# Other places for a decoder step's index-stage buffers, banks and weight halves, and its last normalization on VectorE

## The chip, the cores and the metric

The kernel runs on one core of a Trainium2 chip. Its engines are TensorE (PE, matmuls and transposes into the eight banks of PSUM), VectorE (DVE), ScalarE (ACT, activations by loadable function tables), GpSimd (POOL) and SyncE (SP), which here only issues transfers. Each engine works through its own instruction queue in order; semaphores order the engines against each other. The metric is the time of one execution on the device in microseconds (us).

## What is computed

The reference is one layer of a hybrid decoder for a prompt of 1024 tokens and for 8 sequences with 4 new tokens each and 8192 cached keys. One normalized input is projected by one wide matrix into two branches:

```python
h = rmsnorm(x, g_pre); z = h @ w_in       # qa ka va | qi ki wi | ga | qb kb vb gb
# A: sparse attention
score = sum_h wi[h] * relu(qi[h] @ ki.T / 8)          # 8 index heads, causal
idx = top_k(score, 256)                               # keys kept per query
oa = softmax(qa @ ka[idx].T / 8 + bias) @ va[idx]     # 8 heads, 2 key/value heads
# B: retention, 8 heads, chunks of 128
ob = causal_decay(rope(qb) @ rope(kb).T / 8) @ vb + carried_state
y = concat(silu(ga) * oa, silu(gb) * head_norm(ob)) @ w_out
x = x + rmsnorm(y, g_post)
x = x + (p @ w_ple_up) * sigmoid(x @ w_ple_gate)
```

`head_norm` subtracts each head's mean and multiplies by the reciprocal root of its variance. Outputs are the new `x` for prompt and samples, the new keys, values and index keys, and the final retention states. All is float32; a projection is made of three matmuls on operands split into a high part and a rest (`hi`, `lo`).

## The kernel before

**How orders come about.** The program is traced line by line in one function. A planner then writes each engine's order from estimated costs: at each point an engine takes the first traced instruction that it estimates to be ready, wherever it stands in the program, and buffers and semaphores are assigned along with it. `tc.issue_after(ins)` keeps what its block traces on the engine of `ins` behind `ins` in that queue. Transfers are issued on SP's queue in its order, indirect ones (gathers) on POOL's. A tile of a pool has a `tag` and a number `bufs` of buffers; a new tile of a tag waits until the oldest of its buffers is no longer read.

**Stages.** The span begins with norms and index projections, then index scores of the prompt. From about 155 to 292 us runs the *index stage*, the loop over 8 sequences `b` and 2 halves `a`. It loads a slab of cached index keys (`key_pages`, `kx`, an indirect transfer on POOL, two buffers), transposes it on DVE (L913), multiplies it by the sequence's index queries into a pair of banks (`pox`, L920), takes the relu on ACT (`rl`, L925), and one iteration later sums the heads (`head_sum`: `py`, L881 and L884, copied by ACT into `ys` at L886). In between it steps the prompt's bisection for the top 256 (`bp`: counts on DVE, L740, and on ACT, `js`, L738), and steps `units()`: projection units, each three matmuls times eight input blocks for one group of tokens, in the order queries (`qa0`, `qa1`), keys and values (`kava`), gates (`ga0`, `ga1`), three groups for each of two column halves.

PSUM has, in this phase, two pairs (tag `S`), two banks of tag `b` and two of tag `t`. Projections (`pb`) and head sums (`py`) take `b`; small transposes (`kvt`) and flags take `t`.

A key or value unit copies its projection from the bank into one half of the tile `kvs` (`use_kv`, L466, one buffer) and appends its second part to the list `turn`. The next unit first runs that part (`turn_kv`): transposes of the copy on TensorE (`kvt`, L475), a copy into the other half of `kvs` (L477) and the stores of it (L479, L498). A gate unit applies Silu on ACT (`sga`, L503) and stores the result.

Weights come by `load_w`: two raw halves of four blocks (`wraw`, two buffers), each converted by one cast on ACT (`whi`, L202) and four subtractions on POOL (`wlo`, L203). `lazy=True` returns the conversion as a generator to be stepped later; without it, it is traced at once. `ga0` and `ga1` are traced at once, as units reach them.

**Retention** follows (292 to about 560 us), four head pairs `hp`, with the samples' search for their top 256 beside it. The fourth pair's outputs and gates are stored raw (`yr_d`), with each head's mean and variance kept in `lmv`.

**Attention** of the prompt (about 561 to 735 us) loops over 8 query blocks `qb` and 2 key/value heads `kv`: score matmuls (`sa`, L1835 and L1836), bias, mask and least value on DVE (L1841, `latest[0]`), exponential on ACT (L1845), transposes (`ptp`), copies (`pT`), products with the values (`ob`). Beside it run the samples' attention (`sa` generator: gathers on POOL) and the last pair's normalization, the generator `ln = last_norm()`. It is stepped once ahead of the loop, once in each of the first two blocks, and then three times per `qb` and `kv` from `qb` 2 on. `last_roots` adds the epsilons, takes a root on ACT (L1247) and, a step later, its reciprocal with one Newton round on DVE. Then for each of 9 token blocks: load into `dn` (one buffer, L1791), two steps on normalize on DVE (L1797), multiply by the gate on POOL (L1799), store (L1800).

```python
        for t in range(9):
            a = at.tile([128, 2, 128], F32, tag="dn", bufs=1, name="dn")
            nc.sync.dma_start(a[:n], yr_d[:n, t])
            ...
            nc.gpsimd.tensor_tensor(a[:n, 0, :], a[:n, 0, :], a[:n, 1, :], op=ALU.mult)
            nc.sync.dma_start(yb_d[:n, t, 3, :], a[:n, 0, :])
```

At `qb` 3 the post-norm gains are loaded for the merge (`gpost`, L1814, 512 KB). The **merge** ends the program: output projection (`po`), second norm, gate and embedding.

Of the kernel before, what the change touches and what calls it, by code (L numbers as in the profile page):

```python
# [11 lines left out]
F32 = mybir.dt.float32  # L12
F32R = mybir.dt.float32r
BF16 = mybir.dt.bfloat16
I32 = mybir.dt.int32
# [8 lines left out]
NS = 32  # L24
# [109 lines left out]
def tile_step(ctx: ExitStack, tc: tile.TileContext, I, O):  # L134
# [25 lines left out]
    def bank(name, tag="b"):  # L160
        if tag in kept.get("tags", ()):
            return kept["pool"].tile([128, 512], F32, tag="s", bufs=1, name=name)
        of = psum["apart" if tag == psum["tag"] else "pool"]
        return of.tile([128, 512], F32, tag=tag, bufs=psum["bufs"][tag], name=name)
# [6 lines left out]
    def C(name, rows=128):  # L171
        o, w = _CW[name]
        return cst[:rows, o:o + w]
# [48 lines left out]
    def wcols(*cols):  # L222
        return [(w_in[:, c:c + n], n) for c, n in cols]
# [210 lines left out]
    def key_pages(i):  # L434

        b, a = i // 2, i % 2
        kx = slab("kx").bitcast(F32).rearrange("p a b -> p (a b)")
        paged[0] = nc.gpsimd.indirect_dma_start(
            out=kx[:, :2048], out_offset=None, in_=pages,
            in_offset=bass.IndirectOffsetOnAxis(ap=kidx[:, a * 8 + b:a * 8 + b + 1], axis=0)).ins  # L440
        return kx
# [20 lines left out]

    def use_kv(g, pt, outs, outp, new, then=lambda tk: None):

        st = sx.tile([128, 2, 416], F32, tag="kvs", bufs=1, name="kvs")
        nc.scalar.copy(st[:, 0, :GRP[g][1]], pt[:, :GRP[g][1]])  # L466
        turn.append(lambda: then(turn_kv(g, st, outs, outp, new)))

    def turn_kv(g, st, outs, outp, new):

        t0, n = GRP[g]
        tp = bank("kvt", "t")
        for i in range(0, n, 128):
            rows = min(128, n - i)
            nc.tensor.transpose(tp[:rows, i:i + 128], st[:, 0, i:i + rows], ident)  # L475
        nb = NP[g]
        nc.scalar.copy(st[:, 1, :nb], tp[:, :nb])  # L477
        tk = st[:, 1, :nb].rearrange("p (b c) -> p b c", c=128)
        nc.sync.dma_start(outp[0, 0, t0:t0 + nb].rearrange("(b p) n d -> p b (n d)", p=128), tk)  # L479
        if g == SG:  # L480
            nc.vector.tensor_copy(new, tp[:NS, 384:512])
            nc.sync.dma_start(outs.rearrange("o b t n d -> (o b t) (n d)"), new)
        return tk
# [15 lines left out]

    def use_ga(j, g, pt):  # L500
        t0, n = GRP[g]
        sg = qsp.tile([128, 2, 416], F32, tag="qst", bufs=2, name="sga")
        nc.scalar.activation(sg[:, 0, :n], pt[:, :n], AF.Silu)  # L503
        nc.sync.dma_start(ga_d[:, j, t0:t0 + n], sg[:, 0, :n])

    def units():

        def triple(w, c0, use):
            for g in range(3):
                while turn:  # L510
                    turn.pop(0)()
                proj_b(w, c0, 128, use, (g,))
                yield

        w.extend([load_w("qa0", wcols((QA, 256))), load_w("qa1", wcols((QA + 256, 256)))])
        loads = [("kava", KA), ("ga0", GA), ("ga1", GA + 256), None]
        for i in range(5):
            for a in range(2):
                use = ((lambda g, pt: use_qa(2 * i + a, g, pt)) if i < 2 else
                       (use_ka, use_va)[a] if i == 2 else  # L520
                       (lambda g, pt: use_ga(2 * i - 6 + a, g, pt)))
                yield from triple(w[i], a * 128, use)
            if i < 3:
                w.append(load_w(loads[i][0], wcols((loads[i][1], 256)), late=0 if i else 3))

    w = []
    unit_gen = units()
    tick = [0.0]

# [322 lines left out]

    sp_one = cp.tile([128, 1], F32, name="sp_one")
    nc.gpsimd.memset(sp_one, 1.0)
    bp = bisect_prompt()

    def step(gen, n=1):
# [7 lines left out]
    for up in range(2):  # L865
        nc.vector.tensor_tensor(wst[:, up], wcol[:, :, None].to_broadcast([128, 8, 32]),
                                C(f"wsel{up}")[:, None, :].to_broadcast([128, 8, 32]), op=ALU.mult)
    pn = bank("pn", "t")
    for h in range(8):
        nc.tensor.matmul(pn[:NS, h * 32:h * 32 + 32], qsn[:, h, :], kis, start=True, stop=True)  # L870
# [5 lines left out]
    nc.vector.tensor_tensor(newsc, newsc, C("nfill", 32), op=ALU.add)  # L876
    pend = []
    def head_sum(b, rls):
        py = bank("py")

        last_ = nc.tensor.matmul(py[96:128, :], wst[:, 1, b, :], rls[3], start=True, stop=True)  # L881
        with tc.issue_after(last_.ins):
            for i in range(3):
                nc.tensor.matmul(py[32 * i:32 * i + 32, :], wst[:, i % 2, b, :], rls[i], start=True, stop=True)  # L884
        ys = sx.tile([128, 512], F32, tag="ys", bufs=2, name="ys")
        nc.scalar.copy(ys, py)  # L886
        nc.sync.dma_start(xt_d[b], ys)
        pend.append(lambda: by_key(b, ys))
# [17 lines left out]
    for b in range(8):  # L906
        rls = []
        for a in range(2):
            kx = key_pages(2 * b + a) if b else kxs[a]
            po = pair("pox")  # L910
            kT = (kx[:, 2048:], kx[:, :1024])
            for up in range(2):
                nc.vector.transpose(kT[up], kx[:, up * 1024:up * 1024 + 1024])  # L913
            head = None
            for up in (1, 0):
                for u2 in range(2):
                    for r in range(2):
                        o, rr = 32 * (2 * (r ^ up) + u2), slice(r * 64, r * 64 + 64)
                        with (tc.issue_after(head) if head else ExitStack()):
                            mm = nc.tensor.matmul(po[o:o + 32, up * 512:up * 512 + 512], qbd[rr, b, :],  # L920
                                                  kT[up][rr, u2 * 512:u2 * 512 + 512], start=True, stop=True,
                                                  tile_position=(64 * r, o))
                        head = head or mm.ins
            rl = sx.tile([128, 1024], F32, tag="rl", bufs=3, name="rl")
            nc.scalar.activation(rl, po, AF.Relu)  # L925
            rls += [rl[:, :512], rl[:, 512:]]
            later()
            tickb[0] += 1.25
            while tickb[0] >= 1:
                tickb[0] -= 1  # L930
                step(bp)
            with tc.issue_after(scored[1]):
                unit((2, 2.5, 2, 2)[2 * b + a] if b < 2 else 12.5 / 12)
        pend.append(lambda b=b, rls=rls: head_sum(b, rls))
# [305 lines left out]

    def last_roots():

        v = wif[:, 54:72]
        z = at.tile([128, 18], F32, name="lz")
        nc.vector.tensor_tensor(v.rearrange("p (t h) -> p t h", h=2),
                                lmv[:, :, 1].rearrange("p (t h) -> p t h", h=2), epsn[:, :, 6:8], op=ALU.add)
        nc.scalar.activation(lrs, v, AF.Sqrt)  # L1247
        yield
        with tc.issue_after(latest[0]):
            nc.vector.reciprocal(lrs, lrs)  # L1250
            nc.vector.tensor_tensor(z, lrs, lrs, op=ALU.mult)
            nc.vector.tensor_tensor(z, z, v, op=ALU.mult)
            nc.vector.tensor_scalar(z, z, -0.5, 1.5, op0=ALU.mult, op1=ALU.add)
            nc.vector.tensor_tensor(lrs, lrs, z, op=ALU.mult)

    smask = C("smask", 32)
    bmask = C("bmask")
# [526 lines left out]

    def last_norm():

        yield from last_roots()
        for t in range(9):
            n = 128 if t < 8 else NS
            a = at.tile([128, 2, 128], F32, tag="dn", bufs=1, name="dn")  # L1790
            nc.sync.dma_start(a[:n], yr_d[:n, t])  # L1791
            yield
            yield
            with tc.issue_after(latest[0]):
                for j in range(2):
                    i, js = 2 * t + j, slice(j * 64, j * 64 + 64)
                    nc.vector.tensor_scalar(a[:n, 0, js], a[:n, 0, js], lmv[:n, i, 0:1], lrs[:n, i:i + 1],  # L1797
                                            op0=ALU.subtract, op1=ALU.mult)
            nc.gpsimd.tensor_tensor(a[:n, 0, :], a[:n, 0, :], a[:n, 1, :], op=ALU.mult)  # L1799
            nc.sync.dma_start(yb_d[:n, t, 3, :], a[:n, 0, :])  # L1800
            yield

    latest = [None]
    ln = last_norm()
    caus = C("caus")
    next(ln)

    for qb in range(8):
        qas = qnext
        if qb < 7:  # L1810
            qnext = load_q(qb + 1)
            if qb == 3:
                with tc.issue_after(last_q[0]):
                    nc.sync.dma_start(gpost, I["g_post"].to_broadcast([128, D]))  # L1814
        n = (qb + 1) * 128
# [4 lines left out]
        for kv in range(2):  # L1820
# [26 lines left out]
                more(0.4 + n / 1200)  # L1847
            if qb > 1:
                step(ln)
            elif qb == kv:  # L1850
                next(ln)
            ob = bank("ob", "o")
            for kb in range(qb + 1):
                if kb == 1 and qb > 1:
# [247 lines left out]
```

## Time and profile before

| | |
|---|---|
| median of 3 runs | 974.04 us (972.46 to 976.85) |
| profiled execution | 971.68 us, span 969.9 us |
| mean granted TensorE clock | 0.984 |
| busy: PE, PEld, DVE, ACT, POOL | 95%, 81%, 66%, 47%, 33% |
| moved by DMA | 104.40 MB, 108 GB/s mean |

The span is what the trace covers, from the first to the last instruction; the profiled execution's own time is a little longer. PEld is the loading of stationary operands, which overlaps the matmuls. The granted clock is the share of full speed at which TensorE ran. A row of waits has the engine and line that waited, the one that released it, microseconds in total, times, and the longest. A row of a timeline has start, duration, engine, line, operation, output and inputs, and in brackets the idle time of the engine just ahead and what ended it.

### The profile page before, as it was taken

Reading aid. Unit: us, or ns where it says so; the run is one execution under the profiler, and the core shown is the slowest. Engines: PE = TensorE matmul, PEld = TensorE weight load, DVE = VectorE, ACT = ScalarE, POOL = GpSimd, SP = SyncE. Lnnn points to the kernel's source line nnn. Section 1 sums busy time; section 2 is a strip of 40 time slices with the busy share of each in tenths; the row PEclk is TensorE's granted clock in tenths of the full one; section 3 lists DMA queues with packets and bytes.
Section 4 is the critical chain, followed back from the end, with each engine's and each line's share of the span. In section 5 each row is a group of like instructions: output and inputs, shape, how many; then the busy total and the mean of one; then the engine's idle time right before and its main releaser. Section 6 shows DMA issues by size and latency. Waiting matters only on the chain.

```text
span 969.9 us, 19199 instructions
## 1 busy us (share of the span) xinstructions
PE 917.9 (95%) x7108; PEld 786.8 (81%) x7108; DVE 639.4 (66%) x1898; ACT 458.5 (47%) x1022; POOL 318.8 (33%) x442
## 2 busy tenths in 40 slices
PE   3999999888999999999999988999999999999998
PEld 2988788656779988899889965666668999999998
DVE  6837867878835669978888387877754234943332
ACT  5635654666323886425334284556555334422210
POOL 4205112312415414515344076545204422033300
PEclk8999999988999999999999999999999999999999
DMA  8413224676545110332145445433113222612211
GB/s 261 132 66 83 92 77 153 226 231 197 205 145 124 45 45 24 81 84 63 45 129 164 115 122 167 136 101 103 38 35 87 88 68 77 191 49 94 89 35 39
DMA packets 102129, 104.40 MB, mean 108 GB/s; under 512 B 22002, under 2 KB 92210, under 8 KB 99602
## 3 DMA queue, kind: packets, MB, share of 16 engines
q1 hardware_dynamic: 96274, 76.94, 26.8%
q0 software_dynamic: 5760, 26.22, 8.6%
q8 instruction: 56, 0.92, 0.4%
q14 instruction: 39, 0.32, 0.1%
HBM read 80.38 MB, written 22.76 MB: 106 GB/s over the span
## 4 chain that ended last, share of the span: by engine, by line
PE 54%; DVE 6%; issue 5%; DMA 3%; ACT 2%; POOL 1%; SPq 0%; DVEq 0%; ACTq 0%; POOLq 0%
PE pg L298 3%; PE pg L300 3%; PE pg L299 3%; PE ob L1866 3%; PE ptp L1858 3%; PE po L298 3%; PE po L300 3%; PE po L299 3%; PE pvg L299 2%; PE pvg L298 2%; PE pvg L300 2%; PE sa L1835 2%; PE pqk L298 2%; PE pqk L299 2%; PE pqk L300 2%
## 5 line engine op out<-in xcount | busy, mean ns | idle before, releaser
L1317 POOL DMA_INDIRECT kvs<-in_cache_kv,idx x64 | 67.5, 1054 | 81.8 <-PE pkg L1534 18.5
L298 PE MATMUL pvg<-whi_vgb,xh 128*128 128x256 f32 x256 | 75.2, 294 | 0.5 <-DVE rp L1153 0.5
L299 PE MATMUL pvg<-wlo_vgb,xh 128*128 128x256 f32 x256 | 73.5, 287 | 0.8 <-POOL wlo_vgb L203 0.8
L299 PE MATMUL pqk<-wlo_qkb,xh 128*128 128x256 f32 x256 | 73.9, 289 | 0.0
L298 PE MATMUL pqk<-whi_qkb,xh 128*128 128x256 f32 x256 | 73.8, 288 | 0.1
L300 PE MATMUL pvg<-whi_vgb,xl 128*128 128x256 f32 x256 | 73.7, 288 | 0.0
L300 PE MATMUL po<-whi_o,yTl 128*128 128x256 f32 x256 | 73.1, 285 | 0.4 <-POOL yTl L1914 0.4
L298 PE MATMUL po<-whi_o,yTh 128*128 128x256 f32 x256 | 73.2, 286 | 0.0
L299 PE MATMUL po<-wlo_o,yTh 128*128 128x256 f32 x256 | 72.9, 285 | 0.0
L298 PE MATMUL pg<-whi_g,yTh 128*128 128x256 f32 x256 | 72.8, 285 | 0.0
L300 PE MATMUL pqk<-whi_qkb,xl 128*128 128x256 f32 x256 | 72.8, 284 | 0.0
L300 PE MATMUL pg<-whi_g,yTl 128*128 128x256 f32 x256 | 72.4, 283 | 0.0
L299 PE MATMUL pg<-wlo_g,yTh 128*128 128x256 f32 x256 | 72.3, 283 | 0.0
L1845 ACT ACTIVATE L<-L,mn 128x128 f32<-128x128 f32 (+7 forms) x64 | 49.6, 776 | 22.5 <-DVE mn L1841 22.5
L2057 DVE TENSOR_TENSOR sgm<-pu,sgm 128x256 f32<-128x256 f32 x32 | 13.6, 424 | 64.4 <-PE pu L300 61.1
L203 POOL TENSOR_TENSOR wlo_g<-wraw_g,whi_g 128x256 fp32r<-128x256 f32 x32 | 27.2, 882 | 87.1 <-ACT whi_g L202 87.0
L1858 PEld LDWEIGHTS ptp<-cst,L 128*128 128x128 f32 x288 | 31.6, 142 | 23.8 <-issue 19.4
L298 PEld LDWEIGHTS po<-whi_o,yTh 128*128 128x128 f32 x256 | 49.1, 192 | 2.0 <-issue 1.6
L298 PEld LDWEIGHTS pvg<-whi_vgb,xh 128*128 128x128 f32 x256 | 48.4, 189 | 2.6 <-PE pvg L307 0.8
L298 PEld LDWEIGHTS pg<-whi_g,yTh 128*128 128x128 f32 x256 | 48.8, 191 | 1.6 <-issue 1.2
L569 DVE SCALAR_TENSOR_TENSOR score<-r,wi,score 128x384 f32<-128x384 f32 (+5 forms) x42 | 41.3, 984 | 13.1 <-ACT r L568 10.8
L300 PEld LDWEIGHTS po<-whi_o,yTl 128*128 128x128 f32 x256 | 49.1, 192 | 0.6 <-POOL yTl L1914 0.6
(536 smaller groups left out, 3058.7 us busy)
## 6 DMA issues: line engine op xcount, KB each, us to landing
wraw_qkb<-in_w_in SPq DMA_DIRECT2D x16, 256.0 KB
wraw_vgb<-in_w_in SPq DMA_DIRECT2D x16, 256.0 KB
qas<-qas_d SPq DMA_DIRECT2D x8, 512.0 KB
wraw_o<-in_w_out SPq DMA_DIRECT2D x8, 512.0 KB
xr<-in_x_prompt SPq DMA_DIRECT2D x8, 512.0 KB
wraw_g<-in_w_ple_gate SPq DMA_DIRECT2D x8, 512.0 KB
out_y_prompt<-sgm SPq DMA_DIRECT2D x32, 128.0 KB
qas_d<-qst SPq DMA_DIRECT2D x8, 384.0 KB
```

Of the source, the lines that this page charges most:

```text
L203: nc.gpsimd.tensor_tensor(lo[:, k, :n], raw, hi[:, k, :n].bitcast(F32), op=ALU.subtract)
L298: nc.tensor.matmul(pt[:, :n], ah, hi[:, k, :n], start=(k == 0), stop=False)
L299: nc.tensor.matmul(pt[:, :n], ah, lo[:, k, :n], start=False, stop=False)
L300: nc.tensor.matmul(pt[:, :n], al, hi[:, k, :n], start=False, stop=(k == kc - 1))
L569: nc.vector.scalar_tensor_tensor(sc, r[:, :n], wi[:, qb, h:h + 1], sc if h else place[:, :n], op0=ALU.mult, op1=ALU.add)
L1317: return nc.gpsimd.indirect_dma_start(out=dst, out_offset=None, in_=kvflat, in_offset=bass.IndirectOffsetOnAxis(ap=idx, axis=0))
L1835: nc.tensor.matmul(s[:, :wc], qas[:, h, :], kah[kv][:, c:c + wc], start=True, stop=False)
L1845: behind[0] = nc.scalar.activation(L[:, :n], L[:, :n], AF.Exp, bias=least, scale=-1.0, accum_out=sm[:, i4:i4 + 1])
L1858: nc.tensor.transpose(tp[:, i4 * 128:i4 * 128 + 128], P[i4][:, kb * 128:kb * 128 + 128], ident)
L1866: nc.tensor.matmul(ob[64 * o:64 * o + 64, :256], vtok[:, kb, kv * 64:kv * 64 + 64], pT[:, o * 256:o * 256 + 256], start=(kb == 0), stop=(k ...
L2057: nc.vector.tensor_tensor(sg[:rows], usrc, sg[:rows], op=ALU.mult)
```

## The change

It has four parts.

- Keys and values: `kvs` is split into `kva` (two buffers) and `kvb` (one); the list `turn` holds a count, so that the transposes are traced two units after the copy instead of one. `sga` loses an unused half.
- Gate weights: `ga0` and `ga1` are loaded lazily; at each slab of the index stage, two blocks of each unfinished conversion are traced behind the slab's issue, and what is left is traced ahead of the first gate unit.
- `py` takes a `t` bank. A Silu of one column is traced ahead of the index loop.
- Last pair: `last_roots` takes the reciprocal root on DVE, from a shifted bit pattern and three Newton rounds, a step each. `last_norm` alternates between `dn` and the constant table `slots` (which nothing reads any more by then) and loads a block ahead. The gate product runs on DVE, and the store is traced a step later. The generator is first stepped at `qb` 2. `gpost` is loaded at `qb` 5.

```diff
     def use_kv(g, pt, outs, outp, new, then=lambda tk: None):
-        st = sx.tile([128, 2, 416], F32, tag="kvs", bufs=1, name="kvs")
-        nc.scalar.copy(st[:, 0, :GRP[g][1]], pt[:, :GRP[g][1]])
-        turn.append(lambda: then(turn_kv(g, st, outs, outp, new)))
+        st = sx.tile([128, 416], F32, tag="kva", bufs=2, name="kva")
+        nc.scalar.copy(st[:, :GRP[g][1]], pt[:, :GRP[g][1]])
+        turn.append([2, lambda: then(turn_kv(g, st, outs, outp, new))])
...
-        nc.scalar.copy(st[:, 1, :nb], tp[:, :nb])
+        kb = sx.tile([128, 384], F32, tag="kvb", bufs=1, name="kvb")
+        nc.scalar.copy(kb[:, :nb], tp[:, :nb])
...
             for g in range(3):
-                while turn:
-                    turn.pop(0)()
+                for t in turn:
+                    t[0] -= 1
+                while turn and not turn[0][0]:
+                    turn.pop(0)[1]()
...
         for i in range(5):
+            if i > 2:
+                for _ in w[i][3]:
+                    pass
...
-                w.append(load_w(loads[i][0], wcols((loads[i][1], 256)), late=0 if i else 3))
+                w.append(load_w(loads[i][0], wcols((loads[i][1], 256)), lazy=i > 0, late=0 if i else 3))
+                if i:
+                    halves.append(w[-1][3])
...
+    nc.scalar.activation(sp_two, sp_one, AF.Silu)
...
-        py = bank("py")
+        py = bank("py", "t")
...
             kx = key_pages(2 * b + a) if b else kxs[a]
+            with tc.issue_after(paged[0]):
+                for half in halves:
+                    step(half, 2)
...
     def last_roots():
-        nc.vector.tensor_tensor(v.rearrange("p (t h) -> p t h", h=2),
-                                lmv[:, :, 1].rearrange("p (t h) -> p t h", h=2), epsn[:, :, 6:8], op=ALU.add)
-        nc.scalar.activation(lrs, v, AF.Sqrt)
-        yield
         with tc.issue_after(latest[0]):
-            nc.vector.reciprocal(lrs, lrs)
-            nc.vector.tensor_tensor(z, lrs, lrs, op=ALU.mult)
-            nc.vector.tensor_tensor(z, z, v, op=ALU.mult)
-            nc.vector.tensor_scalar(z, z, -0.5, 1.5, op0=ALU.mult, op1=ALU.add)
-            nc.vector.tensor_tensor(lrs, lrs, z, op=ALU.mult)
+            V.tensor_tensor(v.rearrange("p (t h) -> p t h", h=2),
+                            lmv[:, :, 1].rearrange("p (t h) -> p t h", h=2), epsn[:, :, 6:8], op=ALU.add)
+        V.tensor_scalar(lrs.bitcast(I32), v.bitcast(I32), 1, None, op0=ALU.logical_shift_right)
+        V.tensor_scalar(lrs.bitcast(I32), lrs.bitcast(I32), -1.0, float(0x5F3759DF), op0=ALU.mult, op1=ALU.add)
+        for _ in range(3):
+            yield
+            with tc.issue_after(latest[0]):
+                V.scalar_tensor_tensor(z, lrs, -0.5, lrs, op0=ALU.mult, op1=ALU.mult)
+            V.tensor_tensor(z, z, v, op=ALU.mult)
+            V.scalar_tensor_tensor(lrs, z, 1.5, lrs, op0=ALU.add, op1=ALU.mult)
...
     def last_norm():
+        def load(t):
+            a = rows2[t % 2]
+            n = 128 if t < 8 else NS
+            nc.sync.dma_start(a[:n], yr_d[:n, t])
+            return a[:n]
+        rows2 = [at.tile([128, 2, 128], F32, tag="dn", bufs=1, name="dn"),
+                 C("slots").rearrange("p (a b) -> p a b", a=2)]
+        after = load(0)
         yield from last_roots()
         for t in range(9):
-            a = at.tile([128, 2, 128], F32, tag="dn", bufs=1, name="dn")
-            nc.sync.dma_start(a[:n], yr_d[:n, t])
-            yield
+            a, after = after, load(t + 1) if t < 8 else None
             yield
...
-            nc.gpsimd.tensor_tensor(a[:n, 0, :], a[:n, 0, :], a[:n, 1, :], op=ALU.mult)
-            nc.sync.dma_start(yb_d[:n, t, 3, :], a[:n, 0, :])
+            nc.vector.tensor_tensor(a[:, 0, :], a[:, 0, :], a[:, 1, :], op=ALU.mult)
+            yield
+            nc.sync.dma_start(yb_d[:n, t, 3, :], a[:, 0, :])
             yield
...
-    next(ln)
...
-            if qb == 3:
+            if qb == 5:
                 with tc.issue_after(last_q[0]):
                     nc.sync.dma_start(gpost, I["g_post"].to_broadcast([128, D]))
...
             if qb > 1:
                 step(ln)
-            elif qb == kv:
-                next(ln)
```

More of the change, by code (lines that the diff above doesn't have):

```diff
@@ L474, in turn_kv @@
             rows = min(128, n - i)
-            nc.tensor.transpose(tp[:rows, i:i + 128], st[:, 0, i:i + rows], ident)
+            nc.tensor.transpose(tp[:rows, i:i + 128], st[:, i:i + rows], ident)
         nb = NP[g]
-        nc.scalar.copy(st[:, 1, :nb], tp[:, :nb])
-        tk = st[:, 1, :nb].rearrange("p (b c) -> p b c", c=128)
+        kb = sx.tile([128, 384], F32, tag="kvb", bufs=1, name="kvb")
+        nc.scalar.copy(kb[:, :nb], tp[:, :nb])
+        tk = kb[:, :nb].rearrange("p (b c) -> p b c", c=128)
         nc.sync.dma_start(outp[0, 0, t0:t0 + nb].rearrange("(b p) n d -> p b (n d)", p=128), tk)
@@ L501, in use_ga @@
         t0, n = GRP[g]
-        sg = qsp.tile([128, 2, 416], F32, tag="qst", bufs=2, name="sga")
-        nc.scalar.activation(sg[:, 0, :n], pt[:, :n], AF.Silu)
-        nc.sync.dma_start(ga_d[:, j, t0:t0 + n], sg[:, 0, :n])
+        sg = qsp.tile([128, 416], F32, tag="qst", bufs=2, name="sga")
+        nc.scalar.activation(sg[:, :n], pt[:, :n], AF.Silu)
+        nc.sync.dma_start(ga_d[:, j, t0:t0 + n], sg[:, :n])
     def units():
@@ L523, in units @@
             if i < 3:
-                w.append(load_w(loads[i][0], wcols((loads[i][1], 256)), late=0 if i else 3))
-    w = []
+                w.append(load_w(loads[i][0], wcols((loads[i][1], 256)), lazy=i > 0, late=0 if i else 3))
+                if i:
+                    halves.append(w[-1][3])
+    w, halves = [], []
     unit_gen = units()
@@ L854, in tile_step @@
     nc.gpsimd.memset(sp_one, 1.0)
+    sp_two = cp.tile([128, 1], F32, name="sp_two")
     bp = bisect_prompt()
@@ L1241, in last_roots @@
     def last_roots():
-        v = wif[:, 54:72]
+        V, v = nc.vector, wif[:, 54:72]
         z = at.tile([128, 18], F32, name="lz")
-        nc.vector.tensor_tensor(v.rearrange("p (t h) -> p t h", h=2),
-                                lmv[:, :, 1].rearrange("p (t h) -> p t h", h=2), epsn[:, :, 6:8], op=ALU.add)
-        nc.scalar.activation(lrs, v, AF.Sqrt)
-        yield
         with tc.issue_after(latest[0]):
-            nc.vector.reciprocal(lrs, lrs)
-            nc.vector.tensor_tensor(z, lrs, lrs, op=ALU.mult)
-            nc.vector.tensor_tensor(z, z, v, op=ALU.mult)
-            nc.vector.tensor_scalar(z, z, -0.5, 1.5, op0=ALU.mult, op1=ALU.add)
-            nc.vector.tensor_tensor(lrs, lrs, z, op=ALU.mult)
+            V.tensor_tensor(v.rearrange("p (t h) -> p t h", h=2),
[8 more added lines that the diff above has]
+            V.scalar_tensor_tensor(lrs, z, 1.5, lrs, op0=ALU.add, op1=ALU.mult)
     smask = C("smask", 32)
@@ L1796, in last_norm @@
                     i, js = 2 * t + j, slice(j * 64, j * 64 + 64)
-                    nc.vector.tensor_scalar(a[:n, 0, js], a[:n, 0, js], lmv[:n, i, 0:1], lrs[:n, i:i + 1],
+                    nc.vector.tensor_scalar(a[:, 0, js], a[:, 0, js], lmv[:n, i, 0:1], lrs[:n, i:i + 1],
                                             op0=ALU.subtract, op1=ALU.mult)
-            nc.gpsimd.tensor_tensor(a[:n, 0, :], a[:n, 0, :], a[:n, 1, :], op=ALU.mult)
-            nc.sync.dma_start(yb_d[:n, t, 3, :], a[:n, 0, :])
+            nc.vector.tensor_tensor(a[:, 0, :], a[:, 0, :], a[:, 1, :], op=ALU.mult)
+            yield
+            nc.sync.dma_start(yb_d[:n, t, 3, :], a[:, 0, :])
             yield
```

## Prediction

> **What bounds the kernel now.** I read the page's first two parts, then the windows by stage, then the waits of the stages in which TensorE is not full, then the timelines of single stalls.
>
> ```profile
> span 969.9 us, 19199 instructions
> PE 917.9 (95%) x7108; PEld 786.8 (81%) x7108; DVE 639.4 (66%) x1898; ACT 458.5 (47%) x1022; POOL 318.8 (33%) x442
> ```
>
> TensorE is the bound over the whole span: 917.9 of 969.9 us. The change takes no matmul out, so it can only win TensorE's idle time, 52.0 us, or its lost clock. The windows by stage say where that lies (columns: length, then busy time of PE, PEld, DVE, ACT and POOL, granted clock, DMA share, GB/s).
>
> ```profile
> 164.00:246.00 82.00, 69.61 (x482) 52.28 (x483) 67.73 (x170) 49.55 (x85) 21.69 (x29) 0.92 0.67 218
> 292.00:560.00 268.00, 263.67 (x2258) 242.15 (x2259) 203.44 (x736) 129.60 (x334) 102.90 (x188) 1.00 0.32 83
> 564.00:580.00 16.00, 11.98 (x93) 9.09 (x93) 14.54 (x64) 13.87 (x43) 14.31 (x15) 1.00 0.44 122
> 580.00:600.00 20.00, 20.00 (x173) 13.20 (x171) 15.63 (x65) 11.22 (x33) 15.51 (x15) 1.00 0.57 170
> 608.00:672.00 64.00, 63.67 (x490) 42.79 (x485) 50.51 (x188) 40.07 (x84) 32.52 (x36) 1.00 0.40 114
> ```
>
> The first row is the index stage (key pages, query/key/gate projections, the prompt's bisection): 12.4 us idle, clock 0.92. The second, retention, loses 4.3. Attention begins near 561 and is loose in its first 16 us (4.0 idle, with ACT and DVE nearly full) and again just before 604. Both loose stages are what the diff touches. The waits of the first:
>
> ```profile
> PE kvt L475 <- ACT kvs L466: 3.7, 2, 2.4
> PE py L881 <- ACT sga L503: 3.5, 1, 3.5
> PE pox L920 <- DVE kx L913: 2.2, 1, 2.2
> PE pb L288 <- DVE qst L379: 2.0, 2, 1.3
> ACT kvs L466 <- DMA out_k_prompt<-kvs: 3.7, 2, 2.5
> POOL kx L438 <- PE pox L920: 28.8, 4, 10.1
> ```
>
> **The change part by part: index stage.** *Key/value transposes.* Today a projection group's copy into `kvs` waits for the former group's store out of the same tile (3.7 us on ACT), and the transposes one unit later wait for that copy: 3.7 us of TensorE in two waits. With two `kva` buffers, a separate `kvb`, and the transposes two units late, the copy has a whole unit more and no store in front of it. I take -3.7 (between -3.7 and 0). The wait for the store moves to the second copy (into the single `kvb`), behind which `rl`, `js` and `ys` queue on ACT; the next projection covers it as long as no second tenant of the banks comes within it.
>
> *Bank of the head sums.* `py` takes a `b` bank, which it shares with the projections, so it waits for the gate's activation. That one was late because ACT was held by a count that waited for DVE, and then loaded a table:
>
> ```profile
> 225.89 1.15 ACT L738 ACTIVATE js<-score,W 128x1024 bf16<-128x1024 f32 x1 [3.79 <-DVE W L771]
> 227.15 1.28 ACT L503 ACT_TABLE_LOAD   x1
> 228.44 0.49 ACT L503 ACTIVATE sga<-pb 128x384 f32<-128x384 f32 x1
> 228.00:232.00 4.00, 3.02 (x12) 1.34 (x13) 1.89 (x9) 3.96 (x8) 0.00 (x0) 0.53 0.94 300
> 232.00:236.00 4.00, 4.00 (x15) 3.85 (x15) 3.69 (x12) 3.10 (x6) 0.42 (x1) 0.61 0.95 304
> ```
>
> In a `t` bank `py` no longer waits for the gate: -3.5 (to 0). After that gap the clock falls to 0.53 and 0.61, which costs 0.47 x 3.02 + 0.39 x 4.00 = 3.0 us of matmul time; if the gap goes, so does this: -3.0 (to 0).
>
> *What is late next.* Saving 10.2 leaves 71.8 us of stage for 67.73 us of DVE work that doesn't shrink: 94% full, in order, with page transposes, bisection and PSUM splits behind each other. The waits on DVE (2.2 for pages, 2.0 for query splits) stay, and more will show. The amount is not in the trace; its ends are 0 and 10.2 (all given back). I take the middle, +5.1, since DVE is nearer to full than to its present 83%. Stage: -10.2 + 5.1 = -5.1.
>
> *Gate weights in halves.* The conversions move behind each page's issue on POOL, two at a time, instead of eight in a row:
>
> ```profile
> 178.24 5.57 POOL L203 TENSOR_TENSOR wlo_ga<-wraw_ga,whi_ga 128x256 fp32r<-128x256 f32 x8 [6.69 <-ACT whi_ga L202]
> L290 PE MATMUL pb<-xh,wlo_ga x96: 279/336/548, 220.4 to 289.8; 128*128 128x384 f32 x32, 128*128 128x416 f32 x32, 128*128 128x256 f32 x32
> ```
>
> They end at 183.8 and TensorE first reads them at 220.4: 36.6 us of cover. Page issues stop waiting up to 5.6 us behind them, which only matters where pages are late (in the +5.1). 0. The cost if the cover goes is the slower rival below.
>
> *The early Silu.* It is meant to load the table ahead of the gates. But an instruction whose operands are ready runs as soon as its engine is free, wherever it stands in the program: the memset of its source, from line 854, ran at 0.99 us.
>
> ```profile
> 0.99 0.10 POOL L854 MEMSET sp_one<- 128x1 f32 x1
> 5.85 0.20 ACT L270 ACTIVATE ry_x<-rv_x 128x1 f32<-128x1 f32 x1 [0.22 <-DVE rv_x L267]
> 6.87 0.16 DVE L275 TENSOR_TENSOR ry_x<-ry_x,rz_x 128x1 f32<-128x1 f32 x1
> 8.60 1.28 DVE L599 SCALAR_TENSOR_TENSOR x<-x,ry_x,mask 128x1024 f32<-128x1024 f32 x1 [1.32 <-DMA mask<-in_g_pre]
> ```
>
> I expect it near 2 us too: a load that the root at 5.85 undoes with a second one. That delays the root by 1.28, its chain ends at 7.03 + 1.28 = 8.31, and the scaling waits for `g_pre` until 8.60 anyway: 0 (at most 1.28). The load at 227 then stays, but TensorE no longer stands behind it through `py`: 0.
>
> **Attention.** *Loads a step ahead.* One `dn` buffer serves load, normalization, gate product and store in turn:
>
> ```profile
> 595.49 0.65 SPq L1814 DMA_DIRECT2D gpost<-in_g_post  x1
> 596.23 0.38 SPq L1791 DMA_DIRECT2D dn<-yr_d  x1
> 602.72 0.54 DVE L1797 TENSOR_SCALAR dn<-dn,wi 128x64 f32<-128x64 f32 x2 [6.00 <-DMA dn<-yr_d]
> 603.80 0.77 PE L1835 MATMUL sa<-kahi,qas 128*128 128x512 f32 x1 [3.60 <-DVE mn L1841]
> 604.00:608.00 4.00, 4.00 (x16) 2.14 (x17) 3.68 (x13) 2.56 (x8) 3.27 (x3) 0.61 0.32 90
> ```
>
> The load left behind the 512 KB of `gpost`, DVE stood 6.00 us at its head, the score banks were not drained, TensorE waited 3.60 and then ran at 0.61 (0.39 x 4.00 = 1.6). With two buffers each load has three steps of lead, and `gpost` goes two blocks later, where nothing needs it until the merge. -5.2, the surest term (at least -3.6).
>
> *SP's queue.* The stores now follow a step behind their product, so SP no longer stands at them:
>
> ```profile
> SPq L1800 <- POOL dn L1799: 40.0, 9, 13.3
> SPq L1791 <- DMA yb_d<-dn: 8.7, 6, 2.7
> ```
>
> Queries and gates queued behind those stores are loaded a block ahead; TensorE shows no wait on them: 0. Each load still waits for the store that empties its buffer, now a step old; 2.7 at most and hidden.
>
> *Roots.* Before, ACT switches tables twice for one root:
>
> ```profile
> 569.56 1.28 ACT L1247 ACT_TABLE_LOAD   x1
> 570.86 0.22 ACT L1247 ACTIVATE wi<-wi 128x18 f32<-128x18 f32 x1
> 571.57 1.28 ACT L1845 ACT_TABLE_LOAD   x1
> 571.60 0.65 PE L1534 MATMUL pkg<-cst,kvs 128*128 128x128 f32 x4 [0.55 <-ACT kgT L1535]
> 573.41 1.10 PE L1858 MATMUL ptp<-cst,L 128*128 128x128 f32 x3 [0.68 <-ACT L L1845]
> 576.50 0.66 PE L1534 MATMUL pkg<-cst,kvs 128*128 128x128 f32 x4 [0.61 <-ACT kgT L1535]
> ```
>
> 2 x 1.28 + 0.22 = 2.8 us leave ACT where it is nearly full; TensorE's waits for ACT there sum to 1.84. DVE is as full (14.54 of 16), so I take -1.0 (0 to -1.84). The Trainium skill, "ScalarE: Activation LUTs", section "What ACT_TABLE_LOAD costs", adds a drain of about 1.38 us to each load; by it 5.5 us would leave ACT, and the term would go to its end, -1.84. Here the root starts 0.02 us after its load ends, so the trace shows no drain.
>
> *DVE's new work.* Added: twelve small instructions for the roots (sum, shift, constant, three rounds of three) and nine gate products; removed: six small ones. Their prices:
>
> ```profile
> 572.80 0.17 DVE L1251 TENSOR_TENSOR lz<-wi 128x18 f32<-128x18 f32 x1
> 575.31 0.71 DVE L1252 TENSOR_TENSOR lz<-lz,wi 128x18 f32<-128x18 f32 x1
> L1797 DVE TENSOR_SCALAR dn<-dn,wi x18: 285/310/519, 587.1 to 670.4; 128x64 f32<-128x64 f32 x16, 32x64 f32<-32x64 f32 x2
> ```
>
> The two root rows are the same shape, 0.17 alone and 0.71 while POOL converts. Net 6 x (0.17 to 0.71) + 9 x (0.31 to 0.52) = 3.8 to 8.9 us, spread from about 580 to 700. DVE is free there for 4.4 us in 580 to 600 and 13.5 in 608 to 672. Mostly hidden; +1.0 (0 to +8.9). The Trainium skill, "SBUF — State Buffer", section on the shared port pair, says that DVE with two SBUF inputs and a GpSimd instruction that reads SBUF block each other in full; by it the price would be the 8.9 end wherever POOL computes. The 0.71 row agrees.
>
> **Sum.** -5.1 - 5.2 - 1.0 + 1.0 = -10.3 us. The profiled execution took 971.68 (span 969.9 and 1.78 around it): 961.4. It lies 2.4 below the median of the runs, 974.04; against the median that is 963.7, my forecast.
>
> **The rivals.** *The index stage gives all back.* If DVE paces that stage, PE's idle time only changes its names: attention's -5.2 alone, 968.8. For it: DVE at 67.73 of 82.00. Against: 14 us of it are free, and the two longest waits are on ACT.
>
> *The orders are dealt anew.* Each engine's order is a planner's, from estimated costs, so early edits reorder what follows. The 292 to 560 stage waits for only 4.3 us now; if it and the pages waited 7 us more, twice the longest stall of the index stage, little is left: 971.
>
> *Slower: the gate weights come late.* The last pair of each weight's conversions is now queued on POOL behind a page issue, which waits for its slab until TensorE has read an earlier page: up to 10.1 us. If TensorE gets to the gate projection first, it stands for that wait. Two weights: 20.2 - 10.3 = +9.9, so 984. It decides once the 36.6 us of cover are used up; two such issue waits in a row would take 20.2 of them.
>
> **How the numbers follow.** Forecast 963.7 with its own range 957 to 968.5: 0.50. More (nothing given back): 0.05. Attention alone, 968.8: 0.18, on the edge of what can be told from no change, 0.5% or 4.9 us (969.2): two thirds of it counts as faster. Dealt anew, 971: 0.14. Slower: 0.13. So faster 0.62 (a little under the sum, 0.67, since 968.8 is so near the edge), same 0.24, slower 0.14. The range 956 to 977: down to the stage without give-back (963.7 - 5.1 - 0.84 - 1 = 956.8), up past the two middle rivals; it leaves out the slower one and the extremes.
>
> **What would show it.** Right: no wait of `kvt` on ACT's copy, none of `py` on `sga`; the clock near 1.00 in 225 to 240; DVE above 90% in the index stage; no 6 us wait on `dn`; one table load (not three) between 563 and 575; the early Silu's table load near 2 us and a second root-table load near 6. Wrong: waits of `pb` on `wlo_ga`, of `kvt` or `py` on `ys` or `kvb` copies, longer waits on `kx`, or new idle time between 292 and 560.

## The result, and the profile after

The changed kernel takes 961.46 us (median of 6 runs, 959.65 to 963.53), the kernel before beside it 973.6 (6 runs, 971.54 to 976.85): ratio 0.9878, 95% interval 0.9851 to 0.9904, so 1.2% faster. The profiled execution took 961.63. Its page has the same 7108 matmuls and 5.6 us less TensorE time on them:

```profile
span 959.9 us, 19189 instructions
PE 912.3 (95%) x7108; PEld 781.4 (81%) x7108; DVE 642.1 (67%) x1913; ACT 457.6 (48%) x1022; POOL 308.5 (32%) x433
```

The window of the index stage that the prediction showed for before, and TensorE's waits between 157 and 292 us, in the changed kernel:

```profile
164.00:246.00 82.00, 76.95 (x563) 59.22 (x562) 73.04 (x174) 51.99 (x90) 23.98 (x32) 0.98 0.73 239
```
```profile
PE pox L933 <- issue: 3.5, 2, 2.4
PE pb L288 <- DVE qst L379: 1.8, 2, 1.2
PE pfl L711 <- DVE cf L799: 0.9, 1, 0.9
PE pqk L298 <- DVE sh_qk L312: 0.4, 1, 0.4
PE kvt L475 <- ACT kva L466: 0.2, 1, 0.2
```

81 more matmuls lie in the same 82 us. The wait of `kvt` fell from 3.7 to 0.2, that of `py` on the gate's activation is gone. At the border of retention and attention this profile has waits that the first profile of before shows only in small (1.3 and 0.3). They lie behind the first attention score, so in the table below they count as attention:

```profile
PE ret L1711 <- DVE sbd L1707: 3.4, 1, 3.4
PE ret L1702 <- DVE near L1843: 1.7, 1, 1.7
```

Equal windows no longer hold equal work, so the kernels are compared by stages that TensorE's own instructions bound: the index stage from the first page score (`pox`) to the first projection of retention (`pqk`), retention from there to the first attention score (`sa`), attention from there to the last product with the values (`ob`). The two rows of each kernel are its index and attention stages (columns as in the prediction); those of before come first.

```profile
158.20:290.90 132.70, 119.77 (x845) 91.56 (x848) 100.35 (x220) 64.54 (x108) 37.69 (x52) 0.95 0.63 208
561.60:734.20 172.60, 164.47 (x1259) 107.49 (x1259) 123.85 (x473) 101.47 (x229) 77.67 (x79) 0.99 0.34 98
```
```profile
156.50:277.20 120.70, 114.07 (x846) 86.83 (x848) 100.16 (x220) 63.53 (x108) 38.02 (x52) 0.99 0.70 229
548.40:723.50 175.10, 167.01 (x1259) 109.88 (x1259) 126.36 (x488) 98.45 (x226) 67.17 (x70) 0.97 0.33 96
```

So the index stage won 12.0 us and attention lost 2.5. The 12.0 are 6.3 of idle time (12.9 to 6.6) and 5.7 of TensorE time on the same 845 matmuls (clock 0.95 to 0.99). In a second pair of profiles (e5 and e6) it won 9.3: 3.7 of idle time (12.8 to 9.1) and 5.6 of TensorE time. The same boundaries in every profile taken, in us; "bank" is the head sums' `py` among the transposes' banks, "kv" the key/value tiles apart:

| kernel | bank | kv | attention code | index | retention | attention | ratio to before |
|---|---|---|---|---|---|---|---|
| before | no | no | before | 132.7 | 270.7 | 172.6 | 1 |
| before, second profile (e5) | no | no | before | 132.4 | 271.4 | 172.9 | 1 |
| attention part only (e2) | no | no | changed | 131.1 | 271.8 | 173.3 | 0.9995 |
| bank only (e7) | yes | no | before | 135.4 | 273.2 | 176.8 | 1.0083 |
| changed, without the bank (e4) | no | yes | changed | 134.0 | 270.5 | 178.3 | 1.0042 |
| changed, without kv (e8) | yes | no | changed | 133.6 | 269.6 | 179.9 | 1.0089 |
| bank and kv only (e9) | yes | yes | before | 124.0 | 271.9 | 176.5 | 0.9928 |
| index part only (e1) | yes | yes | before | 120.4 | 269.2 | 175.5 | 0.992 |
| changed | yes | yes | changed | 120.7 | 271.2 | 175.1 | 0.9878 |
| changed, second profile (e6) | yes | yes | changed | 123.1 | 269.3 | 173.7 | 0.9897 |
| changed, no early Silu (e3) | yes | yes | changed | 121.4 | 270.3 | 172.9 | 0.9894 |
| changed, kv one unit late (e10) | yes | yes | changed | 120.3 | 271.1 | 178.8 | 0.9926 |
| changed, two blocks ahead (e11) | yes | yes | changed | 122.7 | 275.0 | 177.3 | 0.9959 |
| changed, whole halves (e12) | yes | yes | changed | 124.8 | 269.9 | 170.6 | 0.9884 |

The profiled execution of e12 ran at a mean granted clock of 0.922 (967.90 us, its other five 954.65 to 960.82), so its stages are read with that in mind. One execution of e1 took 2176.84 us and one of e3 1721.82: the ratios leave them out, and without them the medians given below would be 963.05 and 959.9. The rest of the kernel behind attention takes the same 107.4 to 108.1 us up to the last output product in all fourteen.

### The profile page after: what moved, and what is told of

Its sections match the earlier page's. It is cut to its first block, busy times and chain, and to the rows that moved or that the text cites. A ratio compares the mean times of both kernels' runs of the same rounds, so it can differ in the third digit from the quotient of the medians.

```text
span 959.9 us, 19189 instructions
## 1 busy us (share of the span) xinstructions
PE 912.3 (95%) x7108; PEld 781.4 (81%) x7108; DVE 642.1 (67%) x1913; ACT 457.6 (48%) x1022; POOL 308.5 (32%) x433
## 4 chain that ended last, share of the span: by engine, by line
PE 61%; DVE 13%; issue 11%; DMA 6%; ACT 4%; POOL 2%; SPq 2%; another core or an unknown queue 0%; DVEq 0%; POOLq 0%; ACTq 0%
PE ob L1885 3%; PE ptp L1877 3%; PE pg L298 3%; PE pg L300 3%; PE pg L299 3%; PE po L298 3%; PE po L300 3%; PE po L299 3%; PE pvg L299 2%; PE pvg L298 2%; PE pvg L300 2%; PE sa L1856 2%; PE pb L288 2%; DVE kx L926 2%; PE pb L290 2%
## 5 line engine op out<-in xcount | busy, mean ns | idle before, releaser
L1331 POOL DMA_INDIRECT kvs<-in_cache_kv,idx x64 | 64.3, 1005 | 102.4 <-ACT L L1866 27.6
L2075 ACT ACTIVATE sgm<-pg 128x256 f32<-128x256 f32 x32 | 12.3, 385 | 79.0 <-PE pg L300 74.6
L298 PEld LDWEIGHTS pqk<-whi_qkb,xh 128*128 128x128 f32 x256 | 48.2, 188 | 2.2 <-issue 0.6
```

The costliest lines, as they stand in the source:

```text
L298: nc.tensor.matmul(pt[:, :n], ah, hi[:, k, :n], start=(k == 0), stop=False)
L1331: return nc.gpsimd.indirect_dma_start(out=dst, out_offset=None, in_=kvflat, in_offset=bass.IndirectOffsetOnAxis(ap=idx, axis=0))
```

## The experiments

**The two parts by themselves.** e1 is the kernel before with the diff's hunks up to line 930 alone, e2 with those from line 1240 on alone.

> The index part of the change alone (tiles, banks, lazy halves, early Silu); attention as before. Read from the trace of the changed kernel, this part won 13.7 us by the start of retention and 13.2 by its end; attention then lost 2.6. Theory A (the attention edits do what was predicted of them, -5.2, and a stall at the border of retention and attention, which comes with the earlier arrival, takes it back): the stall of about 7 us between the last retention steps is here too, and so is the 3.6 us wait behind the late dn load; time 965 to 967. Theory B (the attention edits themselves cost 2.5 us): no such stall, 959 to 961, below the changed kernel. Prediction on record: 974.0 - 5.1 = 968.9.

> The attention part of the change alone (roots and gate products on VectorE, loads and stores a step apart, gpost two blocks later); index stage as before. Theory A: -4 to -6 us against before, 968 to 970, with no 6 us wait on dn and no new stall at the border of retention and attention. Theory B: +2 to +3 us, 976, with the stall of 7 us at the border. Prediction on record: -5.2, 968.8.

Measured: e1 963.79 us, ratio 0.992 (0.989 to 0.995); e2 969.96, 0.9995 (0.997 to 1.0019). Neither theory held. On the kernel before, the attention edits neither win 5 us nor cost 2.5; they do nothing that can be measured. The index part carries the gain: 0.8% (0.5 to 1.1%), some 7.8 us, against the prediction's 5.1 just inside the interval. (Its stage of 120.4 us in the table is that of its fastest execution, 958.88 us.) Between e1 and the whole change lie 0.2 to 0.4%, with overlapping intervals, so it stays open whether the attention edits add anything to it. The stall at the border was in both (3.9 and 2.6 us behind `sbd`), and a like one is in e5, so it belongs to neither part. And in e1, with attention's code as before, VectorE's wait for `dn` was 2.5 us, with no wait of TensorE behind it:

```profile
DVE dn L1810 <- DMA dn<-yr_d: 2.5, 2, 1.8
```

**A second profile of each kernel.**

> The kernel before, unchanged, for a second profile. Three things in its first profile carry terms of the prediction or of the comparison: the granted clock of 0.87 in the first 40 us (every later profile has 1.00 there), the 6.00 us wait of VectorE on dn with 3.6 us of TensorE behind it near 604 us (the index part alone, with the same attention code, shows waits on dn of 2.5 us in two and none of TensorE), and the short stall of 1.3 us on sbd at the border of retention and attention (2.6 to 4.2 us in every other profile). Theory C (these three were chance of one execution): clock 1.00 at the start, a wait on sbd of 2.5 to 4 us, attention 173 to 176 us from the first score to the last product instead of 172.6. Theory K (they belong to this kernel's order): the same three again.

> The changed kernel, unchanged, beside the others on one chip, and for a second profile. Expected 0.986 to 0.990 of before; the border's wait on sbd 3 to 4 us again if it belongs to the kernel, below 1.5 us if it is chance.

Measured: e5 970.67 us; e6 961.58, ratio 0.9897 (0.9875 to 0.9919). The second profile of before has a clock of 1.00 in the first 40 us (0.87 in the first) and starts its page scores at 155.7 instead of 158.2. The changed kernel starts them at 156.5 and, in e6, at 157.9: the 1.7 us by which it was ahead in the first pair were chance. The same holds for the prediction's surest term. The first fence has the second profile's rows for the `dn` load behind `gpost`, the second its waits of VectorE on `dn` and of TensorE at the border:

```profile
594.97 0.65 SPq L1814 DMA_DIRECT2D gpost<-in_g_post  x1
595.71 0.38 SPq L1791 DMA_DIRECT2D dn<-yr_d  x1
...
601.37 0.54 DVE L1797 TENSOR_SCALAR dn<-dn,wi 128x64 f32<-128x64 f32 x2 [0.35 <-DMA dn<-yr_d]
```
```profile
DVE dn L1797 <- DMA dn<-yr_d: 0.9, 2, 0.5
...
PE ret L1697 <- issue: 3.2, 2, 2.7
PE ret L1688 <- DVE near L1822: 1.6, 1, 1.6
```

The load is issued in the same place and is used 5.7 us later, against 6.5 in the first profile; but VectorE comes to it only 0.35 us early instead of 6.00. The stage had lost time before that, at the border: 4.8 us of waits there instead of 1.6. Attention takes 172.9 and 172.6 us. One execution waits at the border, the other at `dn`, and the stage is as long. Theory C held for the clock, the border and the wait on `dn`; the stage did not get longer by it.

**The early Silu.**

```
-    nc.scalar.activation(sp_two, sp_one, AF.Silu)
```

> The changed kernel without the early Silu and its tile. The changed kernel was 1.8 us ahead by 157 us, before any other edit acts; the granted clock between 10 and 30 us was 0.83 and 0.66 before and 1.00 after. Theory S (the Silu is worth the 1.8 us, since the instructions of the first 20 us fall otherwise and the clock stays up): clock below 0.9 again between 10 and 30 us and 963 to 964. Rival (the clock at the start is chance, the Silu costs and wins nothing, as predicted): 961 to 962, and one root-table load at the start. Second rival (its absence changes all later orders, by the planner): anything beyond these, with the difference spread over later stages.

Measured: 960.67 us, ratio 0.9894 (0.9854 to 0.9934), clock 1.00 in the first 40 us, page scores from 155.4. No worth of the instruction can be told, as predicted, to within the interval's 4 us either way, and the clock at the start did not come from it: e5 has 1.00 there too. In the changed kernel it ran where the prediction put it, at the very start, with a table load of its own that the root undoes:

```profile
2.25 1.28 ACT L877 ACT_TABLE_LOAD   x1
3.54 0.20 ACT L877 ACTIVATE sp_two<-sp_one 128x1 f32<-128x1 f32 x1
...
5.58 1.28 ACT L270 ACT_TABLE_LOAD   x1
6.87 0.20 ACT L270 ACTIVATE ry_x<-rv_x 128x1 f32<-128x1 f32 x1
```

**The bank and the key/value tiles.** Five kernels: the changed kernel without the one (e4) and without the other (e8), before with the bank alone (e7) and with both alone (e9), and the changed kernel with one unit of delay (e10).

```
e4  -        py = bank("py", "t")              e7  -        py = bank("py")
    +        py = bank("py")                       +        py = bank("py", "t")
e8  -  st = sx.tile([128, 416], F32, tag="kva", bufs=2, ...); turn.append([2, ...
    -  kb = sx.tile([128, 384], F32, tag="kvb", bufs=1, ...)
    +  st = sx.tile([128, 2, 416], F32, tag="kvs", bufs=1, ...); turn.append([1, ...
e9  before with e7's line, and kva, kvb and the delay of 2 as in the change
e10 -        turn.append([2, lambda: ...
    +        turn.append([1, lambda: ...
```

> The changed kernel with the head sums' bank back among the projections' banks. By the prediction's terms this gives back the wait of py on the gate's activation (3.5 us) and the clock that it cost (3.0): 965 to 968, with a wait of py on sga in the list of waits. Rival: with the copies and transposes moved, the activation is no longer late and the bank does not matter: 961 to 962, no such wait.

> The kernel before with one word changed: the head sums' bank with the transposes' banks. Putting it back cost the changed kernel about 16 us, 1.4 to 1.7% (its index stage went from 120.7 to 134.0 us), where the prediction's terms made it 6.5. Theory P (the bank is nearly the whole of the index gain, because head sums and projections in one pair of banks chain ScalarE, TensorE and VectorE one behind the other): index stage 121 to 124 us, time 960 to 963. Theory Q (the bank needs the other edits: kvt and py then share two banks, and kvt waits for the store as before): half of it, 965 to 968, with kvt's waits of some 4 us still there. Prediction's terms: py's wait and its clock, -6.5, with half given back: 968.

> The changed kernel with the key/value tile, its store and its transposes as before (one tile for both copies, transposes one unit late), all else as changed. By the prediction's term the waits of kvt on the copy come back, +3.7: 965 to 966 where the changed kernel has 961.5. Theory P: less, 961 to 963, since the copy is only late while the banks hold ScalarE up.

> The kernel before with two edits together: the head sums' bank with the transposes' banks, and the key/value copies in tiles of their own with transposes two units late. No lazy halves, no early Silu, attention as before. Either of the two without the other left the index stage at 133 to 135 us or made it longer. Theory I (the two work only together, and the rest of the change brings nothing): index stage from the first page score to retention 120 to 123 us, time 960 to 963 where before has 972. Rival H (the lazy halves are needed too): index stage above 126, time 966 or more. Prediction's terms: 974.0 - 10.2 + 5.1, 969 in its terms.

> The changed kernel with the transposes one unit behind the copy instead of two; the tiles stay apart. Theory T (the tiles matter, since the wait for the store is what made the copy late): within 2 us of the changed kernel, 961 to 963. Theory D (the delay matters: one unit is not enough for the copy, since ScalarE has a page's relu, a count and a query copy ahead of it): index stage 128 to 135 us and 970 to 978, with waits of kvt on kva of 2 us or more.

Measured: e4 975.63 us, 1.0042 (1.0018 to 1.0065); e7 979.89, 1.0083 (1.0052 to 1.0114); e8 980.15, 1.0089 (1.0061 to 1.0117); e9 963.74, 0.9928 (0.9897 to 0.996); e10 965.01, 0.9926 (0.99 to 0.9952). Against the theories: e4 and e8 came out slower than anything expected of them (at most 968 and 966), P fell (the bank alone makes the kernel slower), Q fell in its numbers, though `kvt`'s waits are there as it said. Theory I held for the pair, within 1 us of its numbers; that the rest of the change brings nothing is not shown by it, since e9's ratio stands 0.3 to 0.5% above the changed kernel's with intervals that overlap. Without either edit, or with only one, the index stage takes 131 to 135 us; with both, 120 to 125. There is nothing between. The index stage does not need the delay of two units (T against D: 120.3, `kvt` waiting 1.3 in two): what counts there is the separate tiles. T's time of 961 to 963 was missed: e10's ratio stands 0.3 to 0.5% above the changed kernel's, which its index stage does not show; its attention stage was 178.8.

Where the time goes when one edit is missing, by TensorE's waits in that stage (`pox` are page scores, `pb` projections), e7 first, then e4, then e8:

```profile
PE kvt L475 <- ACT kvs L466: 6.3, 3, 3.7
PE pox L920 <- DVE W L746: 3.7, 1, 3.7
PE pox L920 <- issue: 3.5, 1, 3.5
```
```profile
PE pox L933 <- issue: 5.8, 3, 2.3
...
PE pb L288 <- ACT kva L466: 2.0, 1, 2.0
PE pox L933 <- DVE kx L926: 1.9, 1, 1.9
PE pb L288 <- ACT sga L504: 1.5, 1, 1.5
```
```profile
PE pb L288 <- ACT sga L503: 5.8, 1, 5.8
PE pox L932 <- ACT js L745: 4.3, 1, 4.3
PE kvt L475 <- ACT kvs L466: 2.0, 2, 1.3
```

With `py` out of the projections' banks but `kvt` behind the store, TensorE waits at `kvt` and `pox` instead (e7): the wait changes its name. In e8, which also has the bank without the tiles, the longest wait is a projection's for the gate's Silu. With the tiles apart but `py` among the projections (e4), the next projections wait for ScalarE to empty the banks. So the reading is that each edit takes away one of two holds on the same in-order engine, and the other keeps it. The stage times show that it takes both; the two holds are argued from these waits; why the kernels with one edit end above before instead of level with it is not shown. Their attention stages are 4 to 7 us longer than before's, with the two versions of the code that before, the changed kernel, e1, e2 and e3 ran in 172.6 to 175.5.

**The halves of the gate weights.** The changed kernel without `lazy`, `halves` and the loop that steps them behind the page issues:

> The changed kernel with the two gate weights converted at once again, eight conversions in a row on GpSimd, instead of in pairs behind the page issues; all else as changed. The prediction put this edit at 0. Theory Z (0): index stage 120 to 123 us, 960.5 to 963. Rival W (the edit is the 1 to 3 us by which the bank and the key/value tiles alone, at 124.0, stood above the whole change, because eight conversions in a row hold the next page's issue and slow VectorE's small instructions beside them, which took 0.65 to 0.80 us instead of 0.17 in one such stretch): index stage 123.5 to 126, 963 to 966.

Measured: 959.88 us, 0.9884 (0.9858 to 0.991). Theory Z holds by the ratio, which is the changed kernel's: no worth of the edit can be told. W's 963 to 966 did not come; the stage's 124.8 us, within W's numbers, was taken at a clock of 0.88.

**The border.** A version that goes beyond both kernels:

```
-        lead = 8 if hp < 3 else 4
+        lead = 8 if hp < 3 else 2
-                    step(wvg[3], (2 if tb == 1 else 1) if hp < 3 else 3)
+                    step(wvg[3], (2 if tb == 1 else 1) if hp < 3 else 8)
```

> The changed kernel with one thing beyond it: in the last pair of retention heads, two blocks of query/key projections run ahead instead of four, so that more projections stand beside the last steps of the recursion, where every profile but one showed TensorE idle for some 7 us with the clock down to 0.5 to 0.8 behind sbd and sm. The weight halves are converted in one go of eight for it. If that stall is for want of other work, the retention stage is 4 to 8 us shorter and the time 954 to 957; if the planner had these projections there already, or the weight halves come late, 961 to 966.

Measured: 967.71 us, 0.9959 (0.9934 to 0.9983): slower than the changed kernel. Retention grew to 275.0, with the value/gate projections now waiting 4.2 us for ScalarE, and the border's wait moved from `sbd` to the step before it:

```profile
PE pvg L298 <- ACT sg L1179: 4.2, 1, 4.2
PE ret L1702 <- issue: 3.5, 1, 3.5
...
PE ret L1711 <- DVE sbd L1707: 1.4, 1, 1.4
```

Why the border stalls stays open: only e12 has waits as small there as the first profile of before (1.3 and 0.3), with the changed code. No version that was run beats the changed kernel by more than the intervals allow; e3 and e12 can't be told from it and have less code.

## Why the prediction came out, and where it was wrong

The total, 963.7 forecast against 961.46, came out in part by luck: the index stage was priced too low (-5.1; measured -12.0 and -9.3) and attention was given a gain that no run shows (-5.2).

- *`kvt` and `py`, -3.7 and -3.5.* Both waits went as said. But the terms were added as if each edit earned its own. e4, e7 and e8 show that either without the other ends 4 to 9 us above before, and e9 that the two alone carry most of the gain (-0.7%, 7 us).
- *Clock, -3.0: too small.* TensorE's time on the stage's matmuls fell by 5.7 us in the first pair of profiles and by 5.6 in the second. Only the dip after the `py` gap was priced; the stage of before was at 0.95 over its whole length, and 0.99 after.
- *What is late next, +5.1: the step that failed.* Less than that was given back. Of 7.2 us of idle time priced, 6.3 and 3.7 were won, so 0.9 and 3.5 came back in other waits (`pfl` on `cf`, 0.9 and 1.4, is one); with the clock, the stage won 12.0 and 9.3 where the gross gain was put at 10.2. VectorE was taken to be nearly full, from a window of 82 us; over the whole stage it is busy for 100.35 us of 132.7, and for 100.16 of 120.7 after: 83%, with TensorE's waits at `pox` (3.7 before, 3.5 after) and on `qst` (2.0 and 1.8) near where they were. Half of an unknown was no estimate.
- *`dn` a step ahead, -5.2, "the surest term": wrong.* The wait was one execution's. e5 has 0.9 us of waits on `dn` with the same code and the same attention time, and in e2, with all the attention edits, no gain shows. A stall of a loaded stage was read as a cost that adds; by e5 the stage is as long without it.
- *Roots -1.0, VectorE's new work +1.0.* One table load is left of three (550.22), and no wait on the new small operations shows: the twelve took 0.15 to 0.17 us each. The row of 0.17 at 572.80 was read as alone, but conversions of `wlo_o` on GpSimd ran across it (572.15 to 572.92, and from 572.89), so the pair of 0.17 and 0.71 does not show what GpSimd costs. e2's 0.9995 (0.997 to 1.0019) leaves room for -3 to +2 us for all attention edits together, so these two terms can't be told from 0.
- *Early Silu 0, halves 0, SP's queue 0: right*, to within the intervals, by e3 and e12 for the first two; SP's queue was tried only as a part of e2.
- *Rivals.* That the stage gives all back, and that gate weights come late, did not happen: no wait on `wlo_ga` by TensorE. "The orders are dealt anew" was put at 0.14 as the whole outcome and is real as a spread: leaving e12 out, attention took 172.6 to 179.9 us with two versions of its code, and retention, e11's changed code apart, 269.2 to 273.2. The +2.5 of attention in the first pair of profiles (+0.8 in the second) is inside that spread; its cause is not settled.
- *What would show it.* VectorE reached 89% in the window (73.04 of 82), not above 90. The clock between 225 and 229 us still fell to 0.57, behind a `pox` wait of 2.40.

## What to carry to other kernels

Two waits on the same in-order engine are not two terms of a sum: where a bank and a buffer hold the same stream, price the pair, and expect that one fix alone may only rename the wait. Before a stall of one execution becomes the surest term, look for it in a second profile: here a 6 us wait and a clock of 0.87 at the start were gone in the second profile of the same program, which was 1.0 us shorter. Take a stage's fullness from its own ends, not from a window inside it.

## What the runs showed of the hardware

- The same gap may or may not cost clock. Below are the four microseconds with a `pox` wait of 2.40 us and the four behind them, in the changed kernel's first profile and in its second: the same 1.60 us of TensorE work, then a clock of 0.57 in the one and of 1.00 in the other.

```profile
221.00:225.00 4.00, 1.60 (x21) 1.42 (x27) 3.96 (x7) 1.10 (x2) 1.94 (x3) 1.00 0.93 271
225.00:229.00 4.00, 4.00 (x27) 0.98 (x22) 3.72 (x14) 3.02 (x6) 0.95 (x1) 0.57 1.11 344
```
```profile
225.00:229.00 4.00, 1.60 (x16) 1.42 (x15) 3.93 (x8) 1.23 (x2) 2.06 (x3) 1.00 0.91 268
229.00:233.00 4.00, 4.00 (x35) 2.32 (x36) 3.72 (x13) 2.90 (x6) 0.95 (x1) 1.00 1.14 364
```

  The Trainium skill, "TensorE: Matmul & The Clock Gate", section "What's actually happening", has the clock fall after an idle window of some 3.4 us, and the windows run freely, without starting anew with a kernel. A wait of 2.40 us is shorter than that, and one of the two was followed by 0.57 all the same; whether it hung on where in a window the wait fell, the profiles do not show.
- A clock below 1 in the index stage may be partly hidden there: in e12's profile, at 0.88, the same matmuls took 120.89 us instead of 114.07, and the stage 124.80 instead of 120.70, as its idle time was 3.9 instead of 6.6. e12 is another program with orders of its own, so this is a comparison and not a test.

```profile
164.00:288.80 124.80, 120.89 (x845) 89.55 (x848) 98.32 (x221) 63.98 (x108) 37.72 (x52) 0.88 0.66 221
```

- Small VectorE instructions beside a GpSimd conversion can take four to five times as long. In e7 an instruction on 128x6 took 0.76 us while `wlo_ga` was converted and 0.16 without it; the conversions took 0.70 each. Not each is held up: beside a conversion at 180.75 in e7, another on 128x6 took 0.22.

```profile
188.95 0.16 DVE L763 TENSOR_SCALAR far<-W 128x6 int32<-128x6 f32 x1
...
221.62 2.78 POOL L203 TENSOR_TENSOR wlo_ga<-wraw_ga,whi_ga 128x256 fp32r<-128x256 f32 x4
222.32 0.76 DVE L763 TENSOR_SCALAR far<-W 128x6 int32<-128x6 f32 x1
```
